# Second pass of the MLPs: weight operands formed for two neighbouring outputs in one instruction, and their rests on VectorE instead of POOL

## Chip, cores and metric

The kernel runs on one core of a Trainium2 chip. The metric is the device time of one execution in microseconds, as the median of several runs. Before the change it is 2198.36 us (three runs, 2195.66 to 2200.03).

## The reference, cut to what matters

The program is a trunk of two layers: each has a token mixer (latent attention in the first, an mLSTM in the second) and a gated MLP with a short convolution, all in float32. The change concerns the product with `w_down` in both MLPs.

```python
D_MODEL, SEQ, D_FF = 1024, 1024, 2816

def conv_ffn(h, w_up, conv_w, conv_b, w_down):
    a, g = jnp.split(h @ w_up, 2, axis=-1)
    a = lax.conv_general_dilated(a, conv_w[:, None, :], ...) + conv_b
    return (jax.nn.gelu(a, approximate=False) * g) @ w_down

def reference(...):
    for i in range(DEPTH):                      # 2
        ...
        x = x + g_a * y                         # y: the mixer
        h = rms_norm(x) * (1 + sc_f) + sh_f
        x = x + g_f * conv_ffn(h, ffn_w_up[i], ffn_conv_w[i], ffn_conv_b[i], ffn_w_down[i])
    return rms_norm(x, final_norm)
```

## The kernel before

Activations are held transposed, features on the partitions and tokens along the row, in two halves of 512 tokens. Every float32 product is made of three matmuls of a reduced type (`mm3`, L175 to L177): each operand is split into a high part (`hi`) and what is left (`rest`, `lo`), and the three are hi·hi, hi·lo of the activation, and lo·hi with the rest of the weight. So each weight block needs two instructions before TensorE can use it: ScalarE copies it into `hi` (L988), and another engine subtracts, `lo = w − hi` (L989). In `mlp`, `wop` does both for one 128x512 block.

An MLP runs in two passes. The first computes `u = gelu(...)·g` and writes it to HBM (`u_d`). The second, with which the change deals, computes `x += g_f · (u @ w_down)`. Its 22 tiles of 128 inputs form three groups (`DG`): 4 tiles in each of two halves, twice, then 3. Per group the four blocks of the weight (two halves of the outputs by two halves of the inputs) are combined so that seven products replace eight, as Strassen and Winograd do it. The products are called B11, B21, T1, B22, T2, T3, T4 (`ORD`; the third group has another order). B11 and B21 use weight blocks as they are loaded. T1 uses the sum `s` of two blocks (`d_sum`, L1163). B22, T2 and T3 need three subtractions (`derive`, L1171 to L1173, which overwrite `s` and two blocks in place), and T4 a block as loaded.

Each product goes over four outputs p = 0 to 3 (p stands for the output tiles p and p + 4), one after the other: 12 matmuls of 128x512 each (9 in the third group) into one PSUM bank, called `da` for B11, T2, T3 and T4, and `db` for B21, T1 and B22, with four buffers each. After each of these steps a gate (`gate_x`, L294, VectorE) multiplies the bank by g_f and adds it to `x`. I count steps in that order: 28 in a group.

The weight operands are asked for five steps ahead of their product (`LOOK`). `weights(g, p, i)` loads the two blocks of one output half with one DMA of 512 KB, 4 KB in each partition (384 KB in the third group), on SP's queue. Operand tiles are 1024 wide and hold two operands each (`room`), four tiles deep; `sums` keeps two narrow sums in one tile in the same way. The rests are on VectorE but for T3 and T4 in all groups, and B11 and B21 in the second and third: these 40 per MLP are on POOL (GpSimd).

The activations' operands (`operand`, L1138 to L1140, called U) are made three products ahead from tiles `q` that SP loads from `u_d`: per product two subtractions on VectorE (for T1 to T4), two high parts on ScalarE and two rests on VectorE, all 128x1024.

A scheduler puts the instructions of each engine into one fixed order; an engine runs its own order and waits wherever an operand isn't there. So an instruction that waits holds back all that stand behind it on the same engine.

Of the kernel before, what the change touches and what calls it, by code (L numbers as in the profile page):

```python
# [22 lines left out]
HS = 512  # L23
# [30 lines left out]
AHEAD, LOOK, RAWS, MRAWS = 4, (7, 5), 5, 2  # L54
# [43 lines left out]
def trunk_kernel(ctx: ExitStack, tc: tile.TileContext, xT, pos, c_d, cols_d, mod_w, win, winT, w0, w1, wf, wd, out):  # L98
    nc = tc.nc
# [19 lines left out]
    wst, wp, wbufs, wraws = None, None, 3, 2  # L119
# [9 lines left out]
    def block(i, shape, dt, name):  # L129
        return blk.tile(shape, dt, tag=f"b{i}", name=nm(name))  # L130
# [186 lines left out]
    wraw = block(5, [P, 4, 896], F32, "wraw")  # L317
# [501 lines left out]
    for n in range(2 * NH):  # L819
        q, kk, qr, kvu, i, hf, head = args.pop(0)  # L820
# [6 lines left out]
        p = next(sc)  # L827
# [137 lines left out]
    def mlp(px, psC, T, l, u_d, pd, done, cols, extra=None, scaled=None):  # L965
# [17 lines left out]
        def wop(src, eng):  # L983
            if not room:
                t = [wp.tile([P, 1024], F32R, tag=f"w{j}", bufs=wbufs, name=nm(f"w{j}")) for j in ("hi", "lo")]
                room.extend([x[:, i * HS:(i + 1) * HS] for x in t] for i in range(2))
            hi, lo = [v[:, 0:src.shape[-1]] for v in room.pop(0)]
            act.activation(hi, src, AF.Copy)  # L988
            eng.tensor_tensor(lo, src, hi.bitcast(F32), ALU.subtract)  # L989
            return hi, lo  # L990
# [117 lines left out]
        Q, ops, xs, W = {}, {}, [None, None], {}  # L1108
# [35 lines left out]
            for _ in operand(i):  # L1144
                pass

        def weights(g, p, i):

            k0, n = DG[g]
            if (g, p, i) not in W:  # L1150
                t = (pd[0] if i else px).tile([P, 1024], F32, tag=f"raw{i}" if i else "raw", bufs=4 if i else RAWS, name=nm("raw"))
                nc.sync.dma_start(t[:, 0:2 * n * P], wd[l, p + 4 * i, :, k0 * P:(k0 + 2 * n) * P])
                W[g, p, i] = t[:, 0:n * P], t[:, n * P:2 * n * P]
            return W[g, p, i]

        sums = []

        def d_sum(g, p):
            if not sums:
                t = wp.tile([P, 1024], F32, tag="wraw", bufs=wraws, name=nm("wsum"))  # L1160
                sums.extend(t[:, i * HS:(i + 1) * HS] for i in range(2))
            W[g, p, "s"] = sums.pop(0)[:, 0:DG[g][1] * P]
            dve.tensor_tensor(W[g, p, "s"], *weights(g, p, 1), ALU.add)  # L1163
            return W[g, p, "s"]

        def derive(g, p):

            if (g, p, "d") not in W:
                W[g, p, "d"] = True
                sm, (a11, a12), (a21, _) = W[g, p, "s"], weights(g, p, 0), weights(g, p, 1)  # L1170
                dve.tensor_tensor(sm, sm, a11, ALU.subtract)  # L1171
                dve.tensor_tensor(a11, a11, a21, ALU.subtract)
                dve.tensor_tensor(a21, a12, sm, ALU.subtract)  # L1173

        def d_w(g, p, op):
            if op in ("B11", "B21"):
                return wop(weights(g, p, 0)[op == "B21"], pool if g else dve)
            if op == "T1":
                return wop(d_sum(g, p), dve)
            if op == "T4":  # L1180
                return wop(weights(g, p, 1)[1], pool)
            derive(g, p)
            return wop({"B22": weights(g, p, 1)[0], "T2": W[g, p, "s"], "T3": weights(g, p, 0)[0]}[op],
                       pool if op == "T3" else dve)

        bank_a, bank_d, stats = {}, {}, {}

# [49 lines left out]
        for i, (g, op) in enumerate(order):  # L1237
            parts = cols if i == len(order) - 1 else ((0, HS),)
            gen = []
            for t0, width in parts:  # L1240
                for p in range(4):
                    if i == 0 and p in (0, 2):
                        hook(len(seq) - 1, lambda p=p: whole_operand(2 + p // 2))
                    if p == 0 and t0 == 0 and 0 < i and i + 3 < len(order):
                        hook(len(seq) - 1, lambda i=i, gen=gen: gen.append(operand(i + 3)))
                    if p in (0, 2) and t0 == 0 and 0 < i and i + 3 < len(order):
                        hook(len(seq) - 1, lambda gen=gen, p=p: piece(gen[0], 1 + p))
                    if t0 == 0:
                        make = lambda g=g, p=p, op=op: W.setdefault((g, p, op), None) or W.__setitem__(
                            (g, p, op), d_w(g, p, op)) or W[g, p, op]  # L1250
                    else:
                        make = lambda g=g, p=p, op=op: W[g, p, op]
                    seq.append((make, lambda w, i=i, p=p, t0=t0, width=width: d_run(i, p, w, t0, width)))


# [14 lines left out]
    DG = ((0, 4), (8, 4), (16, 3))  # L1270
# [9 lines left out]
    stX, px, stP, psC = open_ffn(1)  # L1280
# [372 lines left out]
    stX, px, stP, psC = open_ffn(2)  # L1653
# [128 lines left out]
```

## Time and profile before

| what | value |
|---|---|
| median of the runs | 2198.36 us (2195.66, 2198.36, 2200.03) |
| span of the profiled execution | 2200.1 us |
| TensorE busy | 2166.5 us, 98% |
| VectorE busy | 1693.1 us, 77% |
| ScalarE busy | 1046.7 us, 48% |
| POOL busy | 178.3 us, 8% |
| second pass of the first MLP, on TensorE | about 904 to 1124 us |
| second pass of the second MLP | about 1965 to 2189 us |

The profile is that of one execution of its own, whose span is the time from its first to its last instruction; it lists no time of that execution beside the span, so the span is what a sum over its rows is set against. PE is TensorE, PEld its loading of weights, DVE VectorE, ACT ScalarE, SP the engine that issues most DMAs. A row of a timeline gives the start, the length of the record, the engine, the line of the kernel, the operation, what it writes and reads, shapes, how many neighbours alike stand in the row, and in brackets the idle time before it with what ended it. Records of one engine overlap, because its instructions are pipelined: what an instruction costs is the distance from its start to the next one's, not its record.

### The profile page before, as it was taken

To read this page: it belongs to the slowest core of one execution; us is meant where nothing else is said; L and a number is where in the kernel's file an instruction comes from. 1 tells how busy PE (TensorE), PEld (TensorE's weight loads), DVE (VectorE), ACT (ScalarE), POOL (GpSimd) and SP (SyncE) were. 2 spreads that over 40 slices of the span, in tenths; PEclk is the share of its full clock that TensorE was granted. 3 is DMA by queue.
4 is the path that set the end of the run, shared out by engine and by line. 5 is a ranking of instruction groups with operands and counts; after the bars stand their busy time and mean duration, and the time that the engine had idled before them with its cause. 6 is when DMAs were issued, how large, how long until landed. Compare 5 with 4: busy or idle time off the path is not lost.

```text
span 2200.1 us, 28740 instructions
## 1 busy us (share of the span) xinstructions
PE 2166.5 (98%) x10557; PEld 1818.0 (83%) x10557; DVE 1693.1 (77%) x2769; ACT 1046.7 (48%) x1812; POOL 178.3 (8%) x216
## 2 busy tenths in 40 slices
PE   9999999999999999999999999999999999999998
PEld 7878888787888888877888888988788888887787
DVE  8877878669878777899973655566887777778997
ACT  6465556446544444543453434344554444453335
POOL 0000000000000000042210111010000000002232
PEclk9999999999999999999999999999999999999999
DMA  8512234832444332542132243444143332245122
GB/s 317 152 50 63 92 109 142 285 125 69 157 139 143 123 125 85 204 151 89 53 121 93 62 131 103 132 157 171 64 144 101 111 120 92 79 163 194 50 80 77
DMA packets 105085, 270.50 MB, mean 123 GB/s; under 512 B 12336, under 2 KB 15984, under 8 KB 104944
## 3 DMA queue, kind: packets, MB, share of 16 engines
q1 hardware_dynamic: 104544, 268.28, 36.9%
q8 instruction: 83, 1.36, 0.3%
q14 instruction: 58, 0.48, 0.1%
q10 hardware_dynamic: 400, 0.39, 0.1%
HBM read 221.53 MB, written 44.47 MB: 121 GB/s over the span
## 4 chain that ended last, share of the span: by engine, by line
PE 85%; DVE 9%; DMA 3%; ACT 2%; issue 1%; POOL 0%; SPq 0%; POOLq 0%; DVEq 0%; ACTq 0%
PE pa L175 7%; PE pa L177 7%; PE pa L176 7%; PE pd L177 3%; PE pd L175 3%; PE pd L176 3%; PE sc L673 3%; PE op L175 3%; PE op L176 3%; PE op L177 2%; PE inp L177 2%; PE da L175 2%; PE inp L175 2%; PE inp L176 2%; PE da L176 2%; PE db L175 2%
## 5 line engine op out<-in xcount | busy, mean ns | idle before, releaser
L988 ACT ACTIVATE whi<-raw 128x512 fp32r<-128x512 f32 (+1 forms) x252 | 147.3, 607 | 243.2 <-PE pb L176 61.0
L988 ACT ACTIVATE whi<-wsum 128x512 fp32r<-128x512 f32 (+1 forms) x224 | 134.0, 617 | 181.8 <-PE pa L176 61.5
L175 PE MATMUL pa<-T,whi 128*128 128x512 f32 x528 | 205.9, 390 | 0.0
L176 PE MATMUL pa<-T,whi 128*128 128x512 f32 x528 | 205.4, 389 | 0.0
L177 PE MATMUL pa<-T,wlo 128*128 128x512 f32 x528 | 205.1, 389 | 0.0
L989 DVE TENSOR_TENSOR wlo<-wsum,whi 128x512 fp32r<-128x512 f32 (+1 forms) x224 | 151.1, 690 | 32.8 <-ACT whi L988 31.5
L989 POOL TENSOR_TENSOR wlo<-raw,whi 128x512 fp32r<-128x512 f32 (+1 forms) x80 | 119.9, 1515 | 401.7 <-ACT whi L988 394.0
L175 PE MATMUL da<-U,whi 128*128 128x512 f32 (+1 forms) x364 | 139.5, 383 | 3.4 <-DVE x L294 3.4
L177 PE MATMUL da<-U,wlo 128*128 128x512 f32 (+1 forms) x364 | 138.4, 383 | 2.0 <-DVE wlo L989 2.0
L176 PE MATMUL da<-U,whi 128*128 128x512 f32 (+1 forms) x364 | 139.2, 382 | 0.0
L989 DVE TENSOR_TENSOR wlo<-raw,whi 128x512 fp32r<-128x512 f32 (+1 forms) x172 | 115.7, 679 | 24.9 <-ACT whi L988 24.9
L167 ACT ACTIVATE whi<-wraw 128x1024 fp32r<-128x1024 f32 x67 | 70.7, 1059 | 117.1 <-PE op L176 59.2
L175 PEld LDWEIGHTS pa<-T,whi 128*128 128x128 f32 x528 | 99.1, 188 | 22.2 <-ACT whi L988 1.2
L177 PEld LDWEIGHTS pa<-T,wlo 128*128 128x128 f32 x528 | 99.1, 188 | 20.6
L176 PEld LDWEIGHTS pa<-T,whi 128*128 128x128 f32 x528 | 99.1, 188 | 20.3
L1140 DVE TENSOR_TENSOR U<-q,U 128x1024 fp32r<-128x1024 f32 x84 | 102.9, 1241 | 14.0 <-ACT U L1139 13.6
L1028 ACT ACTIVATE ct<-a,cols 128x512 f32<-128x512 f32 x88 | 70.8, 808 | 83.9 <-DVE a L1050 47.9
L175 PE MATMUL db<-U,whi 128*128 128x512 f32 x264 | 103.3, 391 | 1.3 <-ACT whi L988 1.3
L168 DVE TENSOR_TENSOR wlo<-wraw,whi 128x1024 fp32r<-128x1024 f32 x67 | 81.7, 1222 | 29.4 <-ACT whi L167 27.2
L177 PE MATMUL db<-U,wlo 128*128 128x512 f32 x264 | 102.9, 390 | 0.0
L176 PE MATMUL db<-U,whi 128*128 128x512 f32 x264 | 102.8, 389 | 0.0
L1139 ACT ACTIVATE U<-q 128x1024 fp32r<-128x1024 f32 x84 | 79.7, 979 | 47.7 <-DVE q L1138 22.2
(378 smaller groups left out, 6097.3 us busy)
## 6 DMA issues: line engine op xcount, KB each, us to landing
raw<-in_wf SPq DMA_DIRECT2D x96, 512.0 KB, 4.0
wraw<-in_w SPq DMA_DIRECT2D x67, 512.0 KB, 3.7
mraw<-in_mod_w SPq DMA_DIRECT2D x56, 512.0 KB, 4.0
ud<-ct SPq DMA_DIRECT2D x88, 256.0 KB, 2.4
q<-ud SPq DMA_DIRECT2D x88, 256.0 KB, 4.6
raw<-in_wd SPq DMA_DIRECT2D x32, 512.0 KB, 6.4
pa<-in_mod_w SPq DMA_DIRECT2D x24, 512.0 KB, 3.7
x<-xd SPq DMA_DIRECT2D x48, 256.0 KB, 4.8
```

Source lines behind the costliest of these rows:

```text
L167: act.activation(hi, raw, AF.Copy)
L168: dve.tensor_tensor(lo, raw, hi.bitcast(F32), ALU.subtract)
L175: pe.matmul(ps, lh, rh, start=first, stop=False, skip_group_check=more)
L176: pe.matmul(ps[:, 0:rl.shape[-1]], lh, rl, start=False, stop=False, skip_group_check=more)
L177: pe.matmul(ps, ll, rh, start=False, stop=last, skip_group_check=more)
L673: pe.matmul(ps[:, cs], a[:, qs if n < 3 else qrs_], b[:, cs], start=n == 0, stop=n == 4)
L988: act.activation(hi, src, AF.Copy)
L989: eng.tensor_tensor(lo, src, hi.bitcast(F32), ALU.subtract)
L1028: act.activation(t, a[:, 2:], AF.Identity, bias=col(f"cb{l}", m), scale=cw(m, 2))
L1139: act.activation(hi, w, AF.Copy)
L1140: dve.tensor_tensor(lo, w, hi.bitcast(F32), ALU.subtract)
```

## The change

`weights` becomes `block_of`: one DMA loads the same one of the four blocks for two neighbouring outputs p and p + 1, where it loaded two blocks for one. It has the same size, but lies in two pieces of 2 KB per partition (1.5 KB in the third group). `two_sum` and `derive` work on such pairs, 128x1024 (128x768 in the third group). `d_two` forms the operands of both outputs with one instruction on ScalarE (L1188) and one on VectorE (L1189), and is called when the first output of a pair is asked for, again five steps ahead. POOL gets none of these rests any more. TensorE's products, the gates and the activations' operands are unchanged.

Per MLP this makes 42 wide high parts of 84 narrow ones on ScalarE. On VectorE 44 narrow rests become 42 wide ones, 12 sums become 6 and 36 subtractions 18; POOL's 40 rests become none.

```diff
-        def weights(g, p, i):
+        def block_of(g, p, b):
 
             k0, n = DG[g]
-            if (g, p, i) not in W:
-                t = (pd[0] if i else px).tile([P, 1024], F32, tag=f"raw{i}" if i else "raw", bufs=4 if i else RAWS, name=nm("raw"))
-                nc.sync.dma_start(t[:, 0:2 * n * P], wd[l, p + 4 * i, :, k0 * P:(k0 + 2 * n) * P])
-                W[g, p, i] = t[:, 0:n * P], t[:, n * P:2 * n * P]
-            return W[g, p, i]
+            if (g, p, b) not in W:
+                t = (pd[0] if b > 1 else px).tile([P, 1024], F32, tag="raw1" if b > 1 else "raw",
+                                                  bufs=4 if b > 1 else RAWS, name=nm("raw"))
+                c0 = (k0 + b % 2 * n) * P
+                v = t[:, 0:2 * n * P]
+                nc.sync.dma_start(v.rearrange("q (p c) -> q p c", p=2),
+                                  wd[l, p + b // 2 * 4:p + b // 2 * 4 + 2, :, c0:c0 + n * P].rearrange("p q c -> q p c"))
+                W[g, p, b] = v
+            return W[g, p, b]
...
-        def d_sum(g, p):
-            if not sums:
-                t = wp.tile([P, 1024], F32, tag="wraw", bufs=wraws, name=nm("wsum"))
-                sums.extend(t[:, i * HS:(i + 1) * HS] for i in range(2))
-            W[g, p, "s"] = sums.pop(0)[:, 0:DG[g][1] * P]
-            dve.tensor_tensor(W[g, p, "s"], *weights(g, p, 1), ALU.add)
+        def two_sum(g, p):
+
+            W[g, p, "s"] = wp.tile([P, 1024], F32, tag="wraw", bufs=wraws, name=nm("wsum"))[:, 0:2 * DG[g][1] * P]
+            dve.tensor_tensor(W[g, p, "s"], block_of(g, p, 2), block_of(g, p, 3), ALU.add)
             return W[g, p, "s"]
...
-                sm, (a11, a12), (a21, _) = W[g, p, "s"], weights(g, p, 0), weights(g, p, 1)
+                sm, a11, a12, a21 = W[g, p, "s"], *[block_of(g, p, b) for b in range(3)]
...
+        def d_two(g, p, op):
+            if op in ("B11", "B21"):
+                src, eng = block_of(g, p, int(op == "B21")), dve
+            elif op == "T1":
+                src, eng = two_sum(g, p), dve
+            elif op == "T4":
+                src, eng = block_of(g, p, 3), dve
+            else:
+                derive(g, p)
+                src = {"B22": block_of(g, p, 2), "T2": W[g, p, "s"], "T3": block_of(g, p, 0)}[op]
+                eng = dve
+            n = src.shape[-1]
+            hi, lo = [wp.tile([P, 1024], F32R, tag=f"w{j}", bufs=wbufs, name=nm(f"w{j}"))[:, 0:n] for j in ("hi", "lo")]
+            act.activation(hi, src, AF.Copy)
+            eng.tensor_tensor(lo, src, hi.bitcast(F32), ALU.subtract)
+            for i in range(2):
+                W[g, p + i, op] = [x[:, i * n // 2:(i + 1) * n // 2] for x in (hi, lo)]
+
         def d_w(g, p, op):
-            if op in ("B11", "B21"):
-                return wop(weights(g, p, 0)[op == "B21"], pool if g else dve)
...
-                       pool if op == "T3" else dve)
+            if (g, p, op) not in W:
+                d_two(g, p, op)
+            return W[g, p, op]
```

How instructions move is seen in the engines' orders. The first place is VectorE's queue in the first MLP's first group, where T1's operands are formed; `wsum` is the sum `s`, `raw` a loaded weight tile, `wlo` a weight's rest, `q` an activation tile, and `x <- db` a gate. Before:

```order
L1138 TENSOR_TENSOR q_8239<-q_8239 128x1024
L294 SCALAR_TENSOR_TENSOR x_8296<-db_8451,modc_79,x_8296 128x512
L1163 TENSOR_TENSOR wsum_8398<-raw_8399 128x512
L1163 TENSOR_TENSOR wsum_8398<-raw_8424 128x512
L1138 TENSOR_TENSOR q_8239<-q_8239 128x1024
L294 SCALAR_TENSOR_TENSOR x_8296<-db_8473,modc_79,x_8296 128x512
L989 TENSOR_TENSOR wlo_8403<-wsum_8398,whi_8402 128x512 x2
L294 SCALAR_TENSOR_TENSOR x_8296<-db_8494,modc_79,x_8296 128x512
L1163 TENSOR_TENSOR wsum_8443<-raw_8444 128x512
L1163 TENSOR_TENSOR wsum_8443<-raw_8468 128x512
```

And now, at the same place:

```order
L1138 TENSOR_TENSOR q_8235<-q_8235 128x1024
L294 SCALAR_TENSOR_TENSOR x_8288<-db_8442,modc_79,x_8288 128x512
L1163 TENSOR_TENSOR wsum_8390<-raw_8391,raw_8393 128x1024
L1138 TENSOR_TENSOR q_8235<-q_8235 128x1024
L294 SCALAR_TENSOR_TENSOR x_8288<-db_8459,modc_79,x_8288 128x512
L1189 TENSOR_TENSOR wlo_8397<-wsum_8390,whi_8396 128x1024
L1163 TENSOR_TENSOR wsum_8432<-raw_8433,raw_8435 128x1024
L294 SCALAR_TENSOR_TENSOR x_8288<-db_8480,modc_79,x_8288 128x512
```

The two narrow sums, each from one loaded tile, have become one wide sum that needs two loaded tiles; the rests follow it at the same distance, behind the same subtraction and gate.

The second place is VectorE's queue some 20 us later, where the operands of T2 and T3 are formed. Before (the rests of T3 are on POOL and don't show):

```order
L1138 TENSOR_TENSOR q_8128<-q_8128 128x1024
L294 SCALAR_TENSOR_TENSOR x_8368<-db_8560,modc_79,x_8368 128x512
L1173 TENSOR_TENSOR raw_8468<-raw_8277,wsum_8443 128x512
L1140 TENSOR_TENSOR U_8592<-q_8128,U_8592 128x1024
L294 SCALAR_TENSOR_TENSOR x_8368<-da_8309,modc_79,x_8368 128x512
L989 TENSOR_TENSOR wlo_8535<-raw_8468,whi_8534 128x512
L989 TENSOR_TENSOR wlo_8575<-wsum_8398,whi_8574 128x512
L989 TENSOR_TENSOR wlo_8612<-wsum_8443,whi_8611 128x512
L1138 TENSOR_TENSOR q_8128<-q_8128 128x1024
```

Now, with the T2 rests `wlo_8551` and `wlo_8586` and the T3 rests `wlo_8619` and `wlo_8657`:

```order
L1189 TENSOR_TENSOR wlo_8551<-wsum_8390,whi_8550 128x1024
L1138 TENSOR_TENSOR q_8128<-q_8128 128x1024
L1189 TENSOR_TENSOR wlo_8586<-wsum_8432,whi_8585 128x1024
L294 SCALAR_TENSOR_TENSOR x_8362<-db_8536,modc_79,x_8362 128x512
L1140 TENSOR_TENSOR U_8568<-q_8128,U_8568 128x1024
L294 SCALAR_TENSOR_TENSOR x_8362<-db_8554,modc_79,x_8362 128x512
L1138 TENSOR_TENSOR q_8128<-q_8128 128x1024
L1189 TENSOR_TENSOR wlo_8619<-raw_8175,whi_8618 128x1024
L294 SCALAR_TENSOR_TENSOR x_8362<-da_8303,modc_79,x_8362 128x512
L1140 TENSOR_TENSOR U_8568<-q_8128,U_8568 128x1024
L294 SCALAR_TENSOR_TENSOR x_8362<-da_8324,modc_79,x_8362 128x512
L1189 TENSOR_TENSOR wlo_8657<-raw_8244,whi_8656 128x1024
```

The T3 rests now stand among the gates and the activations' operands in VectorE's queue.

The third place is TensorE's queue at the step from B22 (`db`) to T2 (`da`) in the same group. Before:

```order
L175 MATMUL da_8332<-U_8420,whi_8574 128x512
L176 MATMUL da_8332<-U_8420,whi_8574 128x512
L175 MATMUL db_8578<-U_8377,whi_8534 128x512
L176 MATMUL db_8578<-U_8377,whi_8534 128x512
L175 MATMUL da_8384<-U_8420,whi_8611 128x512
L176 MATMUL da_8384<-U_8420,whi_8611 128x512
```

Now:

```order
L177 MATMUL db_8519<-U_8371,wlo_8476 128x512
L175 MATMUL db_8536<-U_8371,whi_8515 128x512
L176 MATMUL db_8536<-U_8371,whi_8515 128x512
L175 MATMUL db_8554<-U_8371,whi_8515 128x512
L176 MATMUL db_8554<-U_8371,whi_8515 128x512
L175 MATMUL da_8303<-U_8414,whi_8550 128x512
L176 MATMUL da_8303<-U_8414,whi_8550 128x512
L175 MATMUL da_8324<-U_8414,whi_8550 128x512
L176 MATMUL da_8324<-U_8414,whi_8550 128x512
L175 MATMUL da_8376<-U_8414,whi_8585 128x512
L177 MATMUL db_8536<-U_8371,wlo_8516 128x512
```

Here TensorE starts a few banks with the high parts while rests are still being formed, before and after; T2's second pair (`whi_8585`) now stands ahead of the third B22 output's rest.

More of the change, by code (lines that the diff above doesn't have):

```diff
@@ L1173, in derive @@
                 dve.tensor_tensor(a21, a12, sm, ALU.subtract)
-        def d_w(g, p, op):
-            if op in ("B11", "B21"):
-                return wop(weights(g, p, 0)[op == "B21"], pool if g else dve)
[L1178 to L1183, printed above, removed]
-                       pool if op == "T3" else dve)
+        def d_two(g, p, op):
[15 more added lines that the diff above has]
+                W[g, p + i, op] = [x[:, i * n // 2:(i + 1) * n // 2] for x in (hi, lo)]
+        def d_w(g, p, op):
+            if (g, p, op) not in W:
+                d_two(g, p, op)
+            return W[g, p, op]
         bank_a, bank_d, stats = {}, {}, {}
@@ L1247, in mlp @@
                         hook(len(seq) - 1, lambda gen=gen, p=p: piece(gen[0], 1 + p))
[L1248 to L1252, printed above, removed]
+                    make = lambda g=g, p=p, op=op: d_w(g, p, op)
                     seq.append((make, lambda w, i=i, p=p, t0=t0, width=width: d_run(i, p, w, t0, width)))
```

1 line of the change is left out of this document (removed).

## The prediction

> **What bounds the kernel now.** I read the page's totals first, then its chain, TensorE's waits, windows over the two second passes, and last the timelines around each gap.
>
> ```profile
> span 2200.1 us, 28740 instructions
> PE 2166.5 (98%) x10557; PEld 1818.0 (83%) x10557; DVE 1693.1 (77%) x2769; ACT 1046.7 (48%) x1812; POOL 178.3 (8%) x216
> PE 85%; DVE 9%; DMA 3%; ACT 2%; issue 1%; POOL 0%; SPq 0%; POOLq 0%; DVEq 0%; ACTq 0%
> ```
>
> TensorE is busy for 98% of the span and is most of the chain. The change leaves its matmuls as they are, so it can only give back time in which TensorE stands still, or add such time. The windows cut the second passes at their groups: the first two groups of the first MLP, then of the second (start and end, length, then TensorE, weight loads, VectorE, ScalarE, POOL, granted clock, DMA share, GB/s).
>
> ```profile
> 904.00:988.00 84.00, 82.36 (x360) 67.06 (x360) 78.03 (x92) 34.50 (x49) 23.05 (x14) 1.00 0.55 199
> 988.00:1066.00 78.00, 76.65 (x337) 62.88 (x336) 75.29 (x94) 27.59 (x43) 22.73 (x15) 1.00 0.24 76
> 1965.00:2049.00 84.00, 82.35 (x361) 67.22 (x361) 77.57 (x92) 34.53 (x49) 22.49 (x14) 1.00 0.56 197
> 2049.00:2128.00 79.00, 76.95 (x337) 62.51 (x336) 75.95 (x93) 27.31 (x43) 24.42 (x15) 1.00 0.24 76
> ```
>
> VectorE is busy for 92 to 97% of these stretches, so here it is the second-tightest engine. TensorE's waits, over the whole span:
>
> ```profile
> PE da L175 <- DVE x L294: 3.4, 5, 1.0
> PE da L177 <- DVE wlo L989: 2.0, 2, 1.0
> PE db L175 <- ACT whi L988: 1.3, 2, 0.6
> ```
>
> These are all of the second passes' listed waits: nine, 6.7 us. Their places on TensorE's timeline (start, length of the record, last the idle time and what ended it):
>
> ```profile
> 949.71 0.39 PE L176 MATMUL db<-U,whi 128*128 128x512 f32 x1
> ...
> 950.39 0.39 PE L176 MATMUL da<-U,whi 128*128 128x512 f32 x1
> 951.79 0.50 PE L177 MATMUL da<-U,wlo 128*128 128x512 f32 x1 [1.01 <-DVE wlo L989]
> ...
> 954.43 0.39 PE L176 MATMUL da<-U,whi 128*128 128x512 f32 x1
> 955.45 0.50 PE L175 MATMUL db<-U,whi 128*128 128x512 f32 x1 [0.63 <-ACT whi L988]
> ...
> 993.00 0.39 PE L177 MATMUL da<-U,wlo 128*128 128x512 f32 x1
> 994.21 0.47 PE L175 MATMUL da<-U,whi 128*128 128x512 f32 x1 [0.82 <-DVE x L294]
> ```
>
> The rhythm is (950.39 − 949.71)/3 = 0.227 us from start to start. Against it the first gap costs 951.79 − 950.39 − 0.23 = 1.17, and 0.11 more because the matmul behind it is longer (0.50 for 0.39): 1.28 for a listed wait of 1.01. The second costs 0.79 + 0.11 = 0.90, the third 0.98 + 0.08 = 1.06. So a stall costs its wait and about 0.25: nine make 6.7 + 2.3 = 9.0. The windows say the same: at 0.2267 us a matmul they lose 84 − 360 × 0.2267 = 2.4, then 1.6, 2.2 and 2.6, together 8.8. I take 0.2 per MLP of it as something that no listed wait explains, and leave it there: **8.4 us** can be had.
>
> What makes VectorE late there is seen on its timeline, beside POOL's:
>
> ```profile
> 948.30 1.74 DVE L1171 TENSOR_TENSOR wsum<-wsum,raw 128x512 f32<-128x512 f32 x1
> 949.96 1.77 DVE L989 TENSOR_TENSOR wlo<-wsum,whi 128x512 fp32r<-128x512 f32 x1
> 951.66 0.68 DVE L1172 TENSOR_TENSOR raw<-raw,raw 128x512 f32<-128x512 f32 x1
> ...
> 982.66 2.32 DVE L1140 TENSOR_TENSOR U<-q,U 128x1024 fp32r<-128x1024 f32 x1
> ```
>
> ```profile
> 948.21 2.98 POOL L989 TENSOR_TENSOR wlo<-raw,whi 128x512 fp32r<-128x512 f32 x2 [98.17 <-ACT whi L988]
> ...
> 982.57 5.80 POOL L989 TENSOR_TENSOR wlo<-raw,whi 128x512 fp32r<-128x512 f32 x3 [2.78 <-PE da L177]
> ```
>
> The instructions that coincide with a rest on POOL last 1.7 where the next, without one, lasts 0.68. The T2 rest that TensorE awaits at 951.79 is one of them. The group from 982.57 on POOL stands ahead of the gate wait at 994.21 in the same way.
>
> **The change part by part.** Undisturbed prices on VectorE, by the starts of neighbours:
>
> ```profile
> 936.12 0.68 DVE L1172 TENSOR_TENSOR raw<-raw,raw 128x512 f32<-128x512 f32 x1
> 936.72 1.21 DVE L1140 TENSOR_TENSOR U<-q,U 128x1024 fp32r<-128x1024 f32 x1
> 937.85 0.74 DVE L294 SCALAR_TENSOR_TENSOR x<-db,modc,x 128x512 f32<-128x512 f32 x1
> 938.52 0.68 DVE L1173 TENSOR_TENSOR raw<-raw,wsum 128x512 f32<-128x512 f32 x1
> ```
>
> A narrow tensor_tensor takes 0.60, one of double width 1.13, a gate 0.67. So a pair in one instruction saves only 2 × 0.60 − 1.13 = 0.07.
>
> *VectorE's load.* In a group of four k-tiles stay 14 operand rests and 8 subtractions (1.13 each) and 28 gates: 24.9 + 18.7 = 43.6. Before, there came 16 narrow sums and derived blocks, and 20 rests in the first group or 12 in the second: 36 or 28 × 0.60 = 21.6 or 16.8, in sum 65.2 and 60.4, and beside them 8 or 16 rests on POOL with the stretch they cause. After, 8 wide sums and derived blocks and 14 wide rests: 22 × 1.13 = 24.9, in sum 68.5. TensorE needs 336 × 0.2267 = 76.2 for a group. VectorE thus has 3.3 and 8.1 us more of its own work and no stretch, and keeps 7.7 us free. On average this is nothing for the end, since TensorE's time covers it; what counts is whether it is early enough at each place.
>
> *POOL's 40 rests per MLP* go, and with them the stretch at 948 to 952 and 982 to 992: all nine stalls should go as they stand, −8.4.
>
> *ScalarE* forms 42 wide operands for 84 narrow ones. The nearest rows are the other operands' hi (1052 ns) and the narrow one (624 ns): 2 × 0.62 = 1.25 becomes 1.05, at under half load. No cost on the average, but the later half of a pair is no longer later than the first: T1's first operand waits for its neighbour too.
>
> ```profile
> L988 ACT ACTIVATE whi<-raw 128x512 fp32r<-128x512 f32 x212 | 127.7, 624 | 209.0 <-PE pb L176 61.0 <-DVE raw L1173 43.4 <-PE da L176 28.2
> L1139 ACT ACTIVATE U<-q 128x1024 fp32r<-128x1024 f32 x70 | 72.3, 1052 | 46.3 <-DVE q L1138 22.2 <-DMA q<-ud 8.9 <-PE da L177 7.6
> ```
>
> *New lateness at T1 of the first group.* Before, the first sum needs one raw tile, and T1's first rest is narrow:
>
> ```profile
> 926.92 0.68 DVE L1163 TENSOR_TENSOR wsum<-raw 128x512 f32<-128x512 f32 x1
> 928.18 0.69 DVE L1163 TENSOR_TENSOR wsum<-raw 128x512 f32<-128x512 f32 x1 [0.57 <-DMA raw<-in_wd]
> ...
> 930.58 1.28 DVE L989 TENSOR_TENSOR wlo<-wsum,whi 128x512 fp32r<-128x512 f32 x2
> ...
> 1987.68 1.28 DVE L1163 TENSOR_TENSOR wsum<-raw 128x512 f32<-128x512 f32 x2
> ```
>
> ```profile
> 931.03 0.39 PE L175 MATMUL db<-U,whi 128*128 128x512 f32 x1
> ...
> 931.49 0.40 PE L177 MATMUL db<-U,wlo 128*128 128x512 f32 x1
> ...
> 1992.28 0.39 PE L177 MATMUL db<-U,wlo 128*128 128x512 f32 x1
> ```
>
> The wide sum takes both blocks of two outputs, so both raw tiles must be there: 928.18 as the second one before. Behind it stand in order a subtraction (1.13), a gate (0.67) and the wide rest, whose record I take as 1.21: 928.18 + 1.13 + 1.13 + 0.67 + 1.21 = 932.32. TensorE wants it at 931.49: a new stall of **0.8**. In the second MLP the sum starts at 1987.68, without a wait, and the same sum gives 1991.8 against 1992.28: no stall. A gate behind the waiting sum is late by no more than that and has a spare bank.
>
> When that raw tile lands is the uncertain part, since it now comes as two pieces of 2 KB per partition, not as one of 4 KB. The nearest rows are 256 KB in rows of 2 KB, 4.6 us, and 512 KB, 6.4 us:
>
> ```profile
> q<-ud SPq DMA_DIRECT2D x88, 256.0 KB, 4.6
> raw<-in_wd SPq DMA_DIRECT2D x32, 512.0 KB, 6.4
> ```
>
> So the landing is between 4.6 and 2 × 4.6 = 9.2 us after the issue, that is from 1.8 earlier to 2.8 later at this one place; I take 6.4, as the bytes and the number of transfers are the same. The Trainium skill ("DMA: Bandwidth & Descriptors", section "Why small descriptors are slow (HBM only)") speaks against the change: each packet costs about 3 cycles beside its 32-byte beats, so two packets of 2 KB take 134 cycles where one of 4 KB takes 131; an estimate by that page is 2.3% of 6.4 = 0.15 later, and the forecast would lose 0.15. No run here shows it yet.
>
> *New lateness at T2 of the first group.* From the first wide sum's end (929.3) to the derived blocks of the second pair VectorE has twelve wide instructions and seven gates: 13.6 + 4.7, so 947.6. Then ScalarE forms three operands (B22 and T2 of the first pair, T2 of the second), about 1.0 each: 950.6. TensorE, with T1 starting at 931.03 and 0.8 late, reaches that operand 80 matmuls = 18.1 later, at 950.0: a new stall of about **0.5**. In the second MLP everything on VectorE is 1.3 earlier against TensorE, and TensorE is not late by 0.8: about **0.1**. In groups two and three VectorE runs some 5 us ahead by the load above, and I see none.
>
> *Other edits.* The number and size of the weight DMAs stay the same. On SP's queue three of the second group's raw loads now stand ahead of the loads of activations; they wait for VectorE instructions that stand before the rest that frees the activation tile anyway, so this is covered. If that cover is missing, the activations come later by one wide instruction, 1.13, which the 5 us of lead take. Operand tiles hold two neighbours as before, four deep, so they come free at the same matmul.
>
> *Sum.* −8.4 + 0.8 + 0.5 + 0.1 = −7.0. The profiled span of 2200.1 would become 2193.1. The span is 1.7 above the runs' median of 2198.4, so the median becomes **2191.4**. The runs of before spread by 4.4 us, and 0.2% (4.4 us) is about what a measurement can tell from no change.
>
> **The rivals.** (1) *The lumps eat the gain; no change.* The wide instructions come in lumps at the first group, where VectorE only just keeps up. If the two stalls there stay in both MLPs (1.28 + 0.90, twice: 4.4) and T1's stall is 1.0 in both (2.0), 8.4 − 6.4 = 2.0 remains: 2196.4. For it: VectorE has 3.3 us more of its own work in that group. Against: the stretch that makes those stalls is gone, and the second MLP has its raw tiles in time.
>
> (2) *VectorE is held in order by a rest that waits; slower.* POOL's rests waited for ScalarE's hi, and that for TensorE to free an operand tile. Now VectorE bears those waits, and gates queued behind them come late:
>
> ```profile
> POOL wlo L989 <- ACT whi L988: 196.8, 22, 98.2
> ```
>
> ```profile
> ACT whi L988 <- PE da L176: 26.1, 10, 4.3
> ```
>
> If each of the wide T3 and T4 rests of the long groups (2 products × 2 pairs × 2 groups × 2 MLPs = 16) makes one gate late as now, 3.4/5 + 0.16 = 0.84 each, this is 13.4 − 8.4 = +5.0: 2203.4. It decides once VectorE is held longer than a bank's slack of three steps, 3 × 12 × 0.227 = 8.2 us. Against it: ScalarE's longest wait for TensorE there is 4.3, and POOL's 98.2 is idle time ahead of its first rest.
>
> (3) *The stretch isn't POOL's doing; slower.* If VectorE is slowed by something else, such as its own operands' transfers, the 68.5 us of the second group keep a stretch of 9 to 15 (busy 75.29 less 60.4): up to 83.5 − 76.2 = 7.3 per MLP, so 2198.4 + 14.6 = 2213. Against it: the DMA share of the second group is 0.24, yet the stretch is there; 951.66, the first instruction after POOL's end, is short again. The Trainium skill ("SBUF — State Buffer", section "Who interferes with whom") makes the port that POOL and VectorE share an exclusive lock, which a tensor_tensor with both inputs in SBUF takes for its reads; by it this rival has no chance at all, and the trace agrees at both places quoted.
>
> (4) *The change doesn't do what it says.* The order of instructions has no weight rests left on POOL and half as many on VectorE per output, so I give it nothing.
>
> **How the numbers follow.** Forecast 0.64, rival 1 0.21, rival 2 0.10, rival 3 0.05. The forecast's own range is 2187 to 2196: below, all 9.0 gained, no new stall (2189.4) and about half the spread of the runs, 2.2; above, T1's tile lands 2.8 later in the first MLP, and 1.5 later in the second than it can bear. The range of 8 in 10 reaches on through rival 1 and the edge of rival 2: **2187 to 2200**. Faster by over 0.2% means below 2194.0: nine tenths of the forecast and a tenth of rival 1, 0.60. Slower means above 2202.8: rival 3, and rival 2 for the most part, 0.13. The rest, 0.27, is within 0.2%.
>
> **What would show it.** Right: no VectorE instruction of the second passes stretched beyond 0.75 (narrow) or 1.3 (wide); no waits of TensorE for gates; POOL idle from 904 to the end of the third group; VectorE's busy time in the second group about 1.08 × 68.5 = 74 by its records; one stall of 0.8 at T1's third matmul in the first MLP only, one of about 0.5 some 19 us later. Wrong at the stretch: wide rests of 1.7 or more. Wrong at the walk: stalls of 1 us at T2 in both MLPs. Wrong altogether: waits of TensorE for gates in the T3 and T4 steps, behind a VectorE that idles for ScalarE's hi.

## The result, and the profile after

The changed kernel takes 2193.77 us (median of 21 runs, 2191.74 to 2196.16), the kernel before beside it 2196.68 us (21 runs, 2194.06 to 2201.31). The ratio is 0.9983, with a 95% interval of 0.9977 to 0.9989: 3.7 us faster (2.4 to 5.1), where 7.0 had been forecast. That lies inside the 0.2% that was set as the bound of no change, a case to which the prediction gave 0.27. The profile page's totals after:

```profile
span 2193.9 us, 28407 instructions
PE 2164.5 (99%) x10557; PEld 1818.9 (83%) x10557; DVE 1694.4 (77%) x2717; ACT 1039.1 (47%) x1728; POOL 58.4 (3%) x136
```

POOL has lost 120 us of work, and VectorE has as much as before. The windows over the first two groups of both MLPs, cut as before (TensorE, weight loads, VectorE, ScalarE, POOL, granted clock, DMA share, GB/s):

```profile
904.00:988.00 84.00, 82.75 (x363) 67.33 (x362) 81.11 (x85) 33.10 (x34) 0.00 (x0) 1.00 0.60 199
988.00:1066.00 78.00, 78.00 (x346) 64.59 (x345) 73.23 (x82) 28.29 (x31) 0.00 (x0) 1.00 0.26 76
1965.00:2049.00 84.00, 82.50 (x361) 67.00 (x360) 80.72 (x85) 33.25 (x33) 0.00 (x0) 1.00 0.56 185
2049.00:2128.00 79.00, 79.00 (x350) 65.42 (x349) 74.23 (x83) 26.63 (x29) 0.00 (x0) 1.00 0.25 76
```

In the second group TensorE now works through (346 matmuls in 78 us, 337 before). In the first group it still loses time, almost as much as before. No tensor_tensor of VectorE in the second passes is stretched any more: the longest of 512 columns (narrow) lasts 0.69 there and the longest of 1024 (wide) 1.23. Before, 24 narrow ones were stretched, to 1.80 at most, and 27 wide ones, to 2.32. TensorE's waits in the second passes:

```profile
PE db L177 <- DVE wlo L1189: 1.9, 2, 1.1
PE db L175 <- ACT whi L1188: 0.8, 2, 0.4
```

The nine waits of before are gone, the five for a gate among them; four others have come. Their places on TensorE's timeline:

```profile
931.53 0.39 PE L176 MATMUL db<-U,whi 128*128 128x512 f32 x1
932.76 0.50 PE L177 MATMUL db<-U,wlo 128*128 128x512 f32 x1 [0.84 <-DVE wlo L1189]
...
948.58 0.39 PE L177 MATMUL db<-U,wlo 128*128 128x512 f32 x1
949.37 0.50 PE L175 MATMUL db<-U,whi 128*128 128x512 f32 x1 [0.40 <-ACT whi L1188]
...
1988.90 0.40 PE L176 MATMUL db<-U,whi 128*128 128x512 f32 x1
1990.40 0.50 PE L177 MATMUL db<-U,wlo 128*128 128x512 f32 x1 [1.10 <-DVE wlo L1189]
...
2006.98 0.50 PE L175 MATMUL db<-U,whi 128*128 128x512 f32 x1 [0.40 <-ACT whi L1188]
```

The first and the third are T1's third matmul in the two MLPs. The second and the fourth are the first matmul of B22's third output in the two MLPs. The listed wait is not the whole cost: from 931.53 to 932.76 TensorE loses 1.23 − 0.23 = 1.00, and 0.11 more by the longer matmul behind it.

From the first matmul into a `da` or `db` bank to the last one, the traces give for the second passes of the two MLPs (us):

| kernel | first MLP | second MLP | sum |
|---|---|---|---|
| before | 221.46 | 224.14 | 445.6 |
| changed | 219.20 | 221.19 | 440.4 |
| changed, second trace | 219.28 | 221.29 | 440.6 |
| narrow, no POOL | 217.38 | 219.17 | 436.6 |
| narrow, no POOL, second trace | 217.66 | 219.18 | 436.8 |
| first group narrow | 217.39 | 218.81 | 436.2 |
| first group narrow, second trace | 217.36 | 219.36 | 436.7 |

So 5.2 us were gained where the change works, by one trace of the kernel before. The two profiled spans differ by 6.2; the rest lies in stages that the change leaves alone (the last section shows one). The spans overstate the gain: in every other run the time of the traced execution is 1.7 to 2.0 above its span, so that of the kernel before took about 2202 by this estimate, above the slowest of its 21 runs, 2201.3.

### The profile page after: what moved, and what is told of

Read it like the earlier page. It is cut to its first block, busy times and chain, and to the rows that moved or that the text cites. A ratio compares the mean times of both kernels' runs of the same rounds, so it can differ in the third digit from the quotient of the medians.

```text
span 2193.9 us, 28407 instructions
## 1 busy us (share of the span) xinstructions
PE 2164.5 (99%) x10557; PEld 1818.9 (83%) x10557; DVE 1694.4 (77%) x2717; ACT 1039.1 (47%) x1728; POOL 58.4 (3%) x136
## 4 chain that ended last, share of the span: by engine, by line
PE 87%; DVE 6%; DMA 3%; ACT 2%; issue 2%; POOL 0%; SPq 0%; DVEq 0%; POOLq 0%; ACTq 0%
PE pa L175 7%; PE pa L177 7%; PE pa L176 7%; PE pd L177 3%; PE pd L175 3%; PE pd L176 3%; PE da L175 3%; PE da L176 3%; PE da L177 3%; PE sc L673 3%; PE op L175 3%; PE op L176 3%; PE op L177 3%; PE db L177 2%; PE db L175 2%; PE db L176 2%
## 5 line engine op out<-in xcount | busy, mean ns | idle before, releaser
L988 ACT ACTIVATE whi<-wsum 128x512 fp32r<-128x512 f32 x176 | 107.2, 625 | 127.0 <-PE pa L176 59.6
L989 DVE TENSOR_TENSOR wlo<-wsum,whi 128x512 fp32r<-128x512 f32 x176 | 118.3, 687 | 32.6 <-ACT whi L988 31.2
L988 ACT ACTIVATE whi<-raw 128x512 fp32r<-128x512 f32 x132 | 79.8, 624 | 108.5 <-PE pb L176 61.0
L1188 ACT ACTIVATE whi<-raw 128x1024 fp32r<-128x1024 f32 (+1 forms) x60 | 59.2, 987 | 133.4 <-PE da L176 56.7
L989 DVE TENSOR_TENSOR wlo<-raw,whi 128x512 fp32r<-128x512 f32 x132 | 89.7, 686 | 24.9 <-ACT whi L988 24.9
L175 PE MATMUL inp<-h,whi 128*128 128x512 f32 x256 | 101.0, 395 | 0.0
```

Source lines behind the costliest of these rows:

```text
L175: pe.matmul(ps, lh, rh, start=first, stop=False, skip_group_check=more)
```

## The experiments

Theory A is that of the prediction: VectorE, slowed by POOL's rests, let TensorE wait; moving the rests takes that away. Pairing itself buys nearly nothing, and its lumps cost time in the first group. Theory B: pairing is what buys the time.

**Narrow operands, all rests on VectorE** (the kernel before, edited):

```diff
-                return wop(weights(g, p, 0)[op == "B21"], pool if g else dve)
+                return wop(weights(g, p, 0)[op == "B21"], dve)
-                return wop(weights(g, p, 1)[1], pool)
+                return wop(weights(g, p, 1)[1], dve)
-                       pool if op == "T3" else dve)
+                       dve)
```

> The kernel before, with only the place of the rests changed: all on VectorE, still one output at a time. Theory A (before, TensorE stood still because VectorE was slowed by rests running on POOL; pairing itself buys nearly nothing and costs lumps at the first group): none of the nine stalls of before, no stall at T1 or B22 of the first group either, VectorE's records unstretched, second group's VectorE load 28 x 0.60 + 4 x 0.60 more but under TensorE's 76.2; about 9 us under before, 4 us under the changed kernel, some 2188 to 2190. Theory B (pairing is what buys the time, and unpaired rests are too much for VectorE): stalls at T2 of the first group stay or grow, not faster than the changed kernel, 2194 to 2200.

Measured: 2192.26 us, ratio to before 0.9976 (0.9966 to 0.9986). Its windows:

```profile
904.00:988.00 84.00, 84.00 (x371) 69.39 (x370) 82.43 (x110) 35.78 (x49) 0.00 (x0) 1.00 0.55 193
988.00:1066.00 78.00, 78.00 (x345) 64.59 (x344) 76.67 (x112) 28.61 (x44) 0.00 (x0) 1.00 0.24 76
```

TensorE is busy without a gap in both groups, 371 matmuls in the first where the changed kernel has 363. VectorE with 76.67 us of records in 78 us is fuller than in any other kernel here, and still TensorE waits for none of its weight operands or gates. Theory B falls: without pairs the second passes are 4 us shorter than with them. The time is 2 us above what theory A gave for it, although the second passes have lost the 9 us that it gave; the last section shows where the rest is. The same kernel once more:

> Narrow operands everywhere, all rests on VectorE, once more. No stall in either second pass, as in the first run. If its 3.5 us over the kernel with only the first group narrow was chance in the mLSTM between the MLPs, 2188 to 2190 now; if pairs in the later groups are worth something of themselves, 2192 again.

Measured: 2192.06 us, 0.997 (0.9958 to 0.9982). The second passes are again without a stall at a product of the weights; in both runs one matmul of the first pass, at the start of the second MLP's second pass, waits 0.3 for VectorE. By its time alone this is the case in which pairs in the later groups are worth something of themselves. The table speaks against it: the second passes are as long as in the kernel with only the first group narrow, which comes next. The last section has the stage in which the two differ.

**First group narrow, the others in pairs** (the changed kernel, with the functions of before for g = 0 and their rests on VectorE; `n_w` is the old `d_w`, and the old functions are left out here):

```diff
             if (g, p, op) not in W:
-                d_two(g, p, op)
+                if g == 0:
+                    W[g, p, op] = n_w(g, p, op)
+                else:
+                    d_two(g, p, op)
```

> The first group one output at a time as before (loads too), but with all rests on VectorE; the second and third group in pairs as in the changed kernel. Theory A: the four stalls of the changed kernel at T1 and B22 of the first group (1.1, 0.7, 1.6, 0.7 with their restarts, 4.1 in all) go and nothing else changes; 4 us under the changed kernel, some 2189 to 2190, and the same as narrow operands everywhere on VectorE. Theory B: the first group gets more stalls, 2194 or more.

Measured: 2188.77 us, 0.9962 (0.9949 to 0.9974). The same again, beside the changed kernel:

> The kernel with the first group one output at a time and the others in pairs, all on VectorE, once more beside the changed kernel: 4 to 5 us under it, 2188 to 2190, no stall in either second pass.

> The changed kernel as it is, once more, for a second trace and for a time beside the others of this call. Theory A: stalls of TensorE at T1's third matmul and at B22's third output in both MLPs, about 1.1 and 0.7 each; whether the second MLP's T1 stall is again longer than the first's (1.6 against 1.1) shows if the late x tile there was chance. 2193 to 2195. If the stalls were chance, they are elsewhere or gone.

Measured: 2189.85 us, 0.9961 (0.9949 to 0.9974), against 2194.45 us, 0.998 (0.9971 to 0.9988), for the changed kernel. Its window over the first group has no gap either:

```profile
904.00:988.00 84.00, 84.00 (x372) 69.38 (x371) 82.32 (x106) 35.55 (x45) 0.00 (x0) 1.00 0.55 190
```

The whole shortfall of the changed kernel is thus in its first group, as theory A has it, and this is the fastest version tried, faster than before and than the changed kernel. In its second trace 0.3 are lost at T1's third matmul of the second MLP, without a listed wait. The changed kernel's second trace has its four stalls at the same places, the second MLP's T1 again with the listed wait of 1.1 (and 0.16 two matmuls ahead of it): their places are not chance.

**Pairs, with POOL keeping its rests:**

```diff
-                src, eng = block_of(g, p, int(op == "B21")), dve
+                src, eng = block_of(g, p, int(op == "B21")), pool if g else dve
-                src, eng = block_of(g, p, 3), dve
+                src, eng = block_of(g, p, 3), pool
-                eng = dve
+                eng = pool if op == "T3" else dve
```

> The changed kernel with the rests of T3 and T4 (all groups) and of B11 and B21 (second and third group) put back on POOL, in pairs. Theory A: VectorE's records are stretched again beside POOL's, the gate waits at the start of the second group return (5 to 6 us over both MLPs, with the T2 ones up to 9) on top of the changed kernel's own stalls at T1 and B22; 2199 to 2203, not faster than before. Theory B: VectorE has less to do than in the changed kernel, at or below 2194.

Measured: 2210.6 us, 1.0056 (1.0042 to 1.007), worse than theory A expected. POOL's and VectorE's timelines around 970, and TensorE's behind them:

```profile
970.39 2.51 POOL L1189 TENSOR_TENSOR wlo<-raw,whi 128x1024 fp32r<-128x1024 f32 x1 [5.78 <-PE da L177]
973.24 3.01 POOL L1189 TENSOR_TENSOR wlo<-raw,whi 128x1024 fp32r<-128x1024 f32 x1 [0.34 <-ACT whi L1188]
976.77 2.80 POOL L1189 TENSOR_TENSOR wlo<-raw,whi 128x1024 fp32r<-128x1024 f32 x1 [0.52 <-ACT whi L1188]
```

```profile
970.55 3.44 DVE L1138 TENSOR_TENSOR q<-q,q 128x1024 f32<-128x1024 f32 x1
973.91 0.74 DVE L294 SCALAR_TENSOR_TENSOR x<-da,modc,x 128x512 f32<-128x512 f32 x1
974.58 6.07 DVE L1140 TENSOR_TENSOR U<-q,U 128x1024 fp32r<-128x1024 f32 x2
```

```profile
978.09 0.39 PE L177 MATMUL da<-U,wlo 128*128 128x512 f32 x1
981.36 0.80 PE L175 MATMUL da<-U,whi 128*128 128x512 f32 x1 [2.89 <-DVE x L294]
981.95 0.63 PE L176 MATMUL da<-U,whi 128*128 128x512 f32 x1
982.38 0.63 PE L177 MATMUL da<-U,wlo 128*128 128x512 f32 x1
```

A wide instruction of VectorE that starts beside a wide rest on POOL ends here only after it: 3.44 for 1.22, and 6.07 for two that take 2.35. The gate between them, with one of its inputs in PSUM, keeps its 0.74, but TensorE waits 2.89 for the next one. So pairing made POOL's disturbance longer, not shorter.

**Is it POOL's running, or the moved work?** The changed kernel with idle work on POOL, which takes nothing off VectorE:

```diff
+            if op in ("T3", "T4") or g and op in ("B11", "B21"):
+                w0_ = min(448, n // 2)
+                junk = px.tile([P, 448], mybir.dt.bfloat16, tag="junk", bufs=1, name=nm("junk"))[:, 0:w0_]
+                for i in range(2):
+                    pool.tensor_tensor(junk, src[:, i * n // 2:i * n // 2 + w0_],
+                                       hi[:, i * n // 2:i * n // 2 + w0_].bitcast(F32), ALU.subtract)
```

> The changed kernel, and beside it POOL subtracts the same sources once more (448 of each 512 columns, two instructions for each of the pairs whose rests POOL had before) into a tile that nobody reads; VectorE's and TensorE's work is that of the changed kernel. Theory A: VectorE's records beside these last 1.7 or more again, and gates come late at the start of the second group: 4 to 9 us over the changed kernel, 2198 to 2203. If POOL's running does not slow VectorE: no record over 1.3, the time of the changed kernel within 2 us.

and the same with fills in their place. A subtraction of only 8 columns makes them wait for the same operand; the fills themselves read nothing:

```diff
+                pool.tensor_tensor(junk[:, 0:8], src[:, 0:8], hi[:, 0:8].bitcast(F32), ALU.subtract)
+                for i in range(6):
+                    pool.memset(junk, 0.0)
```

> The changed kernel, and at the places where POOL had its rests it reads 8 columns (to wait for the same operand) and then fills an unread tile six times, without reading. If VectorE is slowed by POOL's reading of SBUF: no VectorE record over 1.3 beside the fills, and the time of the changed kernel. If any work of POOL slows it: records of 1.7 and more, gate waits, 2198 or more.

Measured: 2228.29 us, 1.014 (1.0126 to 1.0154), with the idle subtractions, and 2198.64 us, 1.0004 (0.9995 to 1.0013), with the fills. Groups by line in the first MLP's second pass, the subtractions first, VectorE's wide rests and then POOL's own:

```profile
L1189 DVE TENSOR_TENSOR wlo<-raw,whi 128x1024 fp32r<-128x1024 f32 x19 | 28.2, 1482 | 0.1
...
L1194 POOL TENSOR_TENSOR junk<-raw,whi 128x448 bf16<-128x448 f32 x24 | 46.5, 1939 | 156.5 <-DVE wlo L1189 102.7 <-ACT whi L1188 39.3 <-issue 12.5
```

and with the fills:

```profile
L1189 DVE TENSOR_TENSOR wlo<-raw,whi 128x1024 fp32r<-128x1024 f32 x19 | 23.1, 1216 | 0.3 <-DMA ud<-ct 0.2 <-ACT whi L1188 0.2
...
L1195 POOL MEMSET junk<- 128x448 bf16 x72 | 33.9, 471 | 4.1
```

VectorE's rest goes from a mean of 1.22 to 1.48 with POOL's subtractions, and stays at 1.22 with 34 us of its fills. Of all wide tensor_tensor of the second passes 48 last over 1.3 with the subtractions, up to 2.19, and none with the fills. With the subtractions eight gate waits came back:

```profile
PE da L175 <- DVE x L294: 10.2, 8, 1.6
```

with the fills none. What slows VectorE is POOL reading SBUF, as the Trainium skill has it ("SBUF — State Buffer", section "Who interferes with whom": a DVE instruction with two SBUF inputs contends with a GpSimd instruction that reads SBUF, not with one that only writes); the two runs agree with it. That the kernel with fills is 4.2 us slower than the changed one all the same is not a stall of the second passes: there it has three of the changed kernel's four, and no other, and its second passes are 1.5 us shorter. It lies in TensorE's rhythm in the first passes, which take 421.1 us in each MLP, from their first `pa` matmul to the first `da` matmul, and 417.7 in the changed kernel, although the instructions there are the same: the products on the tile `B` have 0.233 us from start to start instead of 0.227. Why, these runs do not show; an unread tile has been added to a pool there.

The kernel with the subtractions has the same tile and the same 421.1. So of the 34 us by which it is slower than the changed kernel, far more than the 4 to 9 expected, 7 have nothing to do with POOL's reading. Its second passes are 30.9 longer: beside the gates, the matmuls of the norm at the end of each pass wait for VectorE and ScalarE (3.6 and 3.1 us), and behind that TensorE runs at half its rate for some 5 us.

**Which part of the pair costs what in the first group.** T1 narrow, from the paired loads: `two_sum` and T1's hi and rest of the first group work on one output at a time.

> The changed kernel, but the sums and T1 operands of the first group one output at a time (two narrow sums, two narrow hi, two narrow rests for each pair), from the same paired loads; all else in pairs. If the stall at T1 comes from the wide sum and the wide rest, it shrinks by 2 x 0.53 = 1.1, that is to about 0.1 in the first MLP and 0.5 in the second, with B22's stall about as it was: 2 us under the changed kernel. If it comes from the second loaded tile alone (each output of the pair needs both), it stays at 0.8 or more.

Measured: 2206.24 us, 1.0033 (1.0021 to 1.0046): slower, and for a reason that was not foreseen. T1's stall in the first MLP shrank from 1.1 to 0.65, with the second tile as late as in the changed kernel, so of that stall nearly 0.5 is the width and the rest is that a pair needs both tiles. In the second MLP, where the tile landed 0.2 later than in the changed kernel, 1.4 of 1.6 stayed. But the scheduler put a rest (L1140, at 945.18) and a subtraction of the activations on VectorE ahead of the last derived block of the second pair (L1175 here), which starts 3.1 us later, counted from the first `da` matmul, than in the changed kernel:

```profile
948.11 1.22 DVE L1138 TENSOR_TENSOR q<-q 128x1024 f32<-128x1024 f32 x1
949.24 0.74 DVE L294 SCALAR_TENSOR_TENSOR x<-db,modc,x 128x512 f32<-128x512 f32 x1
949.90 1.22 DVE L1175 TENSOR_TENSOR raw<-raw,wsum 128x1024 f32<-128x1024 f32 x1
```

```profile
948.43 0.39 PE L177 MATMUL db<-U,wlo 128*128 128x512 f32 x1
952.26 0.79 PE L175 MATMUL db<-U,whi 128*128 128x512 f32 x1 [3.44 <-ACT whi L1192]
952.85 0.63 PE L176 MATMUL db<-U,whi 128*128 128x512 f32 x1
```

B22's third output waits 3.4 us for it in both MLPs. With pairs the derived blocks of the fourth output are due together with those of the third, one step earlier than narrow ones, and there is no slack: the changed kernel already waits 0.40 here.

B22's and T2's hi and rest narrow, with VectorE's work in the same order:

> The changed kernel, but hi and rest of B22 and T2 of the first group are formed with one instruction for each output; loads, sums and derived blocks stay in pairs, and VectorE's order is the same. TensorE's stall at B22's third output waits for the wide hi on ScalarE (1.06). If it is the width of that instruction, the narrow one (0.62) ends 0.44 earlier and the listed wait of 0.40 goes, in both MLPs (0.67 each with the restart): 1.3 us under the changed kernel, T1's stalls unchanged. If it is the lump of derived blocks on VectorE, the stall stays at 0.3 or more.

Measured: 2192.93 us, 0.9975 (0.9965 to 0.9985), and the second passes 1.5 us shorter than in the changed kernel. Of TensorE's listed waits there only T1's are left:

```profile
PE db L177 <- DVE wlo L1191: 1.4, 2, 0.9
```

The stall at B22 fell from 0.67 to 0.25 in both MLPs: 0.42 of it was the width of ScalarE's instruction. That makes 0.8 of the 1.5; the rest is that T1's stalls were shorter here too, which the edit does not touch. They follow the landing of T1's second tile. Over the eight second passes of the four traces with these loads and sums (the changed kernel twice, with fills, and this one), T1's third matmul has no wait where the tile landed 23.4 us after the first `da` matmul, 0.56 at 24.3, 0.84 to 0.94 at 24.6 to 24.7, and 0.98 to 1.10 at 24.8 to 25.3.

B11 and B21 narrow, in one run:

> The changed kernel, but hi and rest of B11 and B21 of the first group one output at a time, so that the last product tile of the first pass is no longer behind a wide rest on VectorE. If T1's longer stall in the second MLP comes from there (last product late, its store late, so the first T1 weight tiles land late), the last product stands at 11.3 us after the first da matmul instead of 13.0, the second of these tiles lands about 24.0 after it instead of 25.2, and the stall at T1 in the second MLP falls from 1.6 to 1.1 or less. VectorE's order after it changes as in the kernel with narrow T1 (a subtraction and a rest of activations ahead of the last derived block), so B22's second operand is late by about 3.4 again and the time is above that of the kernel before, 2204 to 2208. If the late tiles have another cause, T1's stall in the second MLP stays at 1.6.

Measured: 2203.45 us, with the late B22 operand as expected. The last product of the first pass (the tile whose store to `u_d` goes out ahead of these loads) stood at 11.3 us after the first `da` matmul in both MLPs, as wanted. In the first MLP the second of T1's tiles then landed at 24.0 and the stall was 0.5; in the second it landed at 25.7 and the stall was 1.4, with 0.8 at the matmuls before. So the late product alone is not what makes T1's tiles late in the second MLP.

## Why the prediction was right, and where it was off

The time lies in the forecast's own range, 2187 to 2196 (the kernel before took 2196.7 beside it, 1.7 less than the median that the forecast started from), and the mechanism held: what stretched VectorE went with POOL's rests, and the stalls with it. The gain is about half of what was forecast, because the new stalls of the first group were put too low.

*The stalls of before go (−8.4).* Right: none of the nine is left. The second passes are 5.2 us shorter although new stalls take 4.1, so 9.3 went; the four traces without these new stalls are 8.8 to 9.4 below the one of before. The short gap of 0.2 at the start of each pass stayed.

*VectorE's stretch is POOL's doing.* Right, and shown by the runs with idle subtractions and with fills on POOL. VectorE's records in the second group were forecast at 74 and are 73.2 and 74.2. Rival 3 had no part in it.

*T1 of the first group (+0.8 in the first MLP, none in the second).* The wait in the first MLP is 0.84, as summed. Two things were off. The stall costs 1.1, because I had added about 0.25 for the restart to each stall that went and to none that came. And in the second MLP the step failed that read "the sum starts at 1987.68, without a wait": that row holds two narrow sums, the second of which began 0.6 later. In that trace the second tile landed at 1988.1, too late for a wide sum at 1987.68, and no wait showed it because the first sum needed one tile only. Yet from 1988.1 on the same sum gives 1992.2 against 1992.28, still no stall. The larger error is that the tile was taken to land as early as before. In the changed kernel the second tile landed 25.2 us after the first `da` matmul, 23.7 before, and VectorE waited:

```profile
1986.19 1.22 DVE L1163 TENSOR_TENSOR wsum<-raw,raw 128x1024 f32<-128x1024 f32 x1 [0.98 <-DMA raw<-in_wd]
```

The stall there is 1.4, and 0.3 at the matmuls just before. The load itself takes hardly longer, 6.98 us from issue to landing where it took 6.82 (the forecast took 6.4). But SP issues it 18.2 us after the first `da` matmul, where it was 16.9. Why SP issues it later is open: the last product as the only cause was tried and fell, and in that run these loads stood in SP's queue behind transfers that had not landed yet (1.3 us of listed waits).

*T2 of the first group (+0.5 and +0.1).* The walk over VectorE's queue held (derived blocks of the second pair at 947.6 by the sum; ScalarE's copy that waits for them starts at 948.25, in a trace whose pass begins 0.27 later). But the operand that TensorE waits for first is B22's of the second pair, eight matmuls ahead of T2's, and one of ScalarE's three copies is enough:

```profile
948.25 1.06 ACT L1188 ACTIVATE whi<-raw 128x1024 fp32r<-128x1024 f32 x1 [6.75 <-DVE raw L1173]
949.22 1.99 ACT L1188 ACTIVATE whi<-wsum 128x1024 fp32r<-128x1024 f32 x2
```

The stall is 0.67 in each MLP. In the second it is not smaller, because T1's tile was late there.

*Sum.* −9.3 + 4.1 = −5.2 in place of −8.4 + 1.4 = −7.0. The failed terms are the new stalls, mis-sized by 2.7: 1.0 of it the restarts of four stalls, most of the rest T1 in the second MLP, which was put at nothing. Rival 1 thus came half true: the lumps took nearly half of the gain, at T1 and B22, not at the places of the old stalls. Rival 2 did not happen, since no gate wait is left.

*Loads in two pieces.* The four tiles behind one another land 1.26 us apart in the kernel before and 1.32 apart in the changed one (second MLP, 1986.8 to 1990.6 and 1984.7 to 1988.7). Over all traces the mean is 1.26 in the ten first groups loaded in rows of 4 KB (1.25 to 1.27) and 1.31 in the sixteen loaded in pieces of 2 KB (1.26 to 1.41), 4% more. The estimate by the Trainium skill ("DMA: Bandwidth & Descriptors", section "Why small descriptors are slow (HBM only)") was 2.3%; the sign agrees, the size is larger.

## What to carry to other kernels

Two engines that read the same memory can cost more together than one alone: before giving work to an idle engine, look whether the records of its neighbour grow beside it. Forming operands in pairs halves the number of instructions but makes the first of a pair wait for what the second needs, so it belongs, if anywhere, where the producer runs ahead; the first group of these passes is not that place. A new stall is priced like an old one, with its restart, and a row that groups neighbours hides when the second of them began.

## What else the runs showed

After a stall of about 3 us TensorE ran at half its rate for a while: behind the wait of 2.89 at 981.36 its matmuls stand 0.43 apart instead of 0.23, until 984.5, and the granted clock from 981.0 to 984.6 is 0.55. This is why the stalls of 3.4 to 3.5 cost 5 to 7 us each in the kernels where they occur. It also happens in stages without any change. In the mLSTM between the MLPs, windows from 1300 to 1400 us of the kernel before, of the narrow kernel without POOL, and of the one with the first group narrow:

```profile
1300.00:1400.00 100.00, 98.27 (x575) 87.05 (x574) 56.63 (x116) 32.00 (x68) 8.06 (x9) 0.98 0.43 142
```

```profile
1300.00:1400.00 100.00, 98.11 (x593) 87.94 (x593) 56.15 (x115) 31.49 (x68) 8.47 (x9) 0.98 0.46 145
```

```profile
1300.00:1400.00 100.00, 98.84 (x616) 89.22 (x616) 57.01 (x117) 30.97 (x67) 8.83 (x9) 1.00 0.47 149
```

The first two have a granted clock of 0.98 there, the third 1.00; the second traces of the last two kernels have 0.98 and 1.00 again. From the end of the first MLP's second pass to the start of the second MLP's first pass it takes 421.6, 422.6 and 419.8 us, and 422.8 and 420.6 in the second traces of the last two. So the narrow kernel and the one with only the first group narrow, equal within 0.6 in the second passes, differ by 2 to 3.5 us in the median, and 2 to 3 us of difference stand in a stage that neither changes. Which program meets the half clock there was the same in two traces each; why, is not shown, and pairing is not shown to be worth anything.
